# A two-layer hybrid trunk on one core: low parts of the conv weights by ScalarE and an adding transfer, p·v of two heads in turns, and the work between the attention units spread anew

## The chip, the cores and the metric

The kernel runs on one core of one Trainium2 chip. The metric is the device time of one execution in microseconds: 1858.16 us, the median of three runs (1857.69 to 1860.25). Engines are named as the profile names them: PE is TensorE (matrix products; PEld is its loading of weights), DVE is VectorE, ACT is ScalarE, POOL is GpSimd, SP issues the loads. Each engine takes its instructions in the order of its own queue. "Granted clock" is the share of TensorE's full clock that the throttle lets through: 1.00 is 2.4 GHz and 0.50 is 1.2 GHz.

## The reference

A sequence of 512 tokens of width 1024 goes through two layers. Each layer is: SwiGLU half step, a mixer, SwiGLU half step, each with an RMSNorm before it, shift and scale from a conditioning vector, and a gated residual add. All data are float32. The two mixers are the places of the change:

```
def conv_mixers(h, w_in, conv_a_w, conv_a_b, ln_a_g, ln_a_b, conv_b_w, w_out):   # layer 0
    z = h @ w_in                                      # 1024 x 2560
    a_val, a_gate, b_gate, c_gate, b_val = split(z)   # 512 columns each
    a = a_val * sigmoid(a_gate)
    a = causal_depthwise_conv(a, conv_a_w) + conv_a_b # 31 taps
    a = silu(group_layer_norm(a, 8, ln_a_g, ln_a_b))
    bb = b_gate * causal_depthwise_conv(c_gate * b_val, conv_b_w)   # 3 taps
    return concatenate([a, bb]) @ w_out

def pool_moba_mixers(...):                            # layer 1
    u, q, k, v = split(h @ w_in)                      # 512 columns each, 8 heads of 64
    pooled = multiscale_pool(u, ...)                  # trailing means of 2, 4, 8, 16 and a 128x128 product
    att = moba_attention(q, k, v)                     # causal softmax(q k' - slope * distance) v
    return concatenate([pooled, att]) @ w_out
```

With 512 tokens and blocks of 256 each query sees all keys before it, so the attention is plain causal attention with a linear bias.

## The kernel before

Activations lie transposed, channels on the 128 partitions and the 512 tokens along the row. A weight tile of 128x1024 (an **item**: 128 output columns, 8 steps over the inputs) is split into a high part, its rounding to the short float type that TensorE takes at full rate, and a low part, the rest. Each step of a product is then three matmuls of 128x512 into one PSUM bank (`mac`, L299 to L301): high times high, high times low of the activations, low times high. One item is 24 matmuls.

`run` walks a plan that is written out by hand. Before the step that uses item n it emits the splits of up to three items ahead (`AHEAD`), as far as the ring of four weight buffers (`W_BUFS`) allows. `split` has two instructions: ACT rounds the raw tile (`whi`, L284), and DVE subtracts (`wlo <- raw - whi`, L286); for items marked `pool_low` POOL subtracts. Raw tiles are loaded by SP (`load`, L268 or L261) into four buffers, each with two items.

**The conv stage** (`build`): items z[0] to z[3] belong to the step across the norm before it; then come z[3] to z[19] one after the other, each followed by `conv_tick`, which emits five taps of the 31-tap convolution on DVE (L1126, one multiply-add each) and three on ACT and POOL (ACT multiplies, `tp`, L1114, three buffers; POOL adds, L1115). The order of the items is sigmoid gate and value (`ag`, `av`) of four channel groups, then for two pairs of groups `cg`, `bv`, `bgate`. What an item leaves behind is put to DVE and ACT too: `bv` multiplies (`cb`, L1051), ACT makes the first of three taps (`yb`, L1054), DVE the two others (L1058). The normalisation over groups of 64 channels (`group_norm`) goes in three steps over PE, DVE, ACT and POOL (L1166 to L1192). After z[19] the first four items of the output product (`zo[0]` to `zo[3]`) are done step by step: steps 4 and 5 of each item, then 6, 7, 0, 1, 2, 3 of all four. Of these, zo[1] to zo[3] are `pool_low`.

**The attention stage**: 8 heads of 4 query blocks are 32 units. Unit n emits the scores of its block (two matmuls, L1345 and L1346, softmax on DVE and ACT), the transposes of the probabilities of unit n-3 (L1372, copied by ACT to `pta` and `ptb`, two buffers each), and, where unit n-6 was the last of a head, that head's product p·v (`product`, L1393: four float32 matmuls of 64 output rows, 512, 384, 256 and 128 columns; even heads write rows 0 to 63 of a bank, odd heads rows 64 to 127). After two heads ACT and DVE split the bank into high and low part for the output product. Between the units stand other matmuls, so that PE has work while a softmax runs: `FILL` says in which units half an item of the input product stands (12 matmuls), `PARTS` in which units steps of the first four output items stand.

Of the kernel before, what the change touches and what calls it, by code (L numbers as in the profile page):

```python
# [8 lines left out]
F32 = mybir.dt.float32  # L9
# [5 lines left out]
P = 128  # L15
D = 1024
S = 512
# [25 lines left out]
class Item:  # L43


    def __init__(self, raw, cut, shape, post=None, rhs=None, korder=None, store=None):
        self.raw, self.cut, self.shape = raw, cut, shape
        self.post, self.rhs = post, rhs
        self.korder, self.store = korder, store
        self.hi = self.lo = self.ps = None  # L50
        self.left = 0
        self.pool_low = self.late = self.hold = False


class Pair:
# [13 lines left out]
class Trunk:  # L69
# [183 lines left out]
    def load(self, r):  # L253
        n = 1
        for s in r.shape[1:]:
            n *= s
        t = self.raw.tile([P, 2048], F32, name="raw", tag="raw")[:, 0:n]
        if isinstance(r.src, tuple):
            r.tile = t.rearrange("p (g k c) -> p g k c", g=2, k=ND)
            for g in range(2):  # L260
                self.nc.sync.dma_start(r.tile[:, g], r.src[g])  # L261
        elif len(r.shape) == 4:
            r.tile = t.rearrange("p (a b c) -> p a b c", a=r.shape[1], b=r.shape[2])
            for b in range(r.shape[2]):
                self.nc.sync.dma_start(r.tile[:, :, b, :], r.src[:, :, b, :])
        else:
            r.tile = t.rearrange("p (a b) -> p a b", a=r.shape[1])
            self.nc.sync.dma_start(r.tile, r.src)  # L268

    def split(self, it):  # L270
        nk, m = it.shape
        src = it.cut(it.raw.tile)
        if it.store is None:
            parts = [[p.tile([P, 1024], F32R, name=n, tag=n)[:, 0:nk * m].rearrange(
                "p (a b) -> p a b", a=nk) for p, n in ((self.wp, "whi"), (self.wp, "wlo"))]]
            step = nk
        else:
            parts = [[t.rearrange("p (a b) -> p a b", b=m) for t in pair] for pair in it.store]
            step = S // m
        it.hi, it.lo = [], []  # L280
        for i, (hi, lo) in enumerate(parts):
            w = src[:, i * step:(i + 1) * step, :]
            n = w.shape[1]
            self.nc.scalar.copy(hi[:, 0:n, :], w)  # L284
            eng = self.nc.gpsimd if it.pool_low else self.nc.vector
            low = lambda eng=eng, lo=lo, hi=hi, w=w, n=n: eng.tensor_tensor(  # L286
                lo[:, 0:n, :], w, hi[:, 0:n, :].bitcast(F32), op=ALU.subtract)
            if it.hold:
                self.held.append(low)
            else:  # L290
                low()
            it.hi += [hi[:, a, :] for a in range(n)]
            it.lo += [lo[:, a, :] for a in range(n)]
# [350 lines left out]
    def t_rhs(self, k):  # L644
        return self.th[k], self.tl[k]

    def pair(self, src, nk, posts, apart=False, **kw):
# [4 lines left out]
        r = Raw([P, nk, 256], src, 2)  # L652
        return [Item(r, (lambda t, j=j: t[:, :, j * P:(j + 1) * P]), (nk, P), post=posts[j], **kw)
                for j in range(2)]

    def ffn_items(self, l, s):
        nc, a = self.nc, self.a
# [360 lines left out]
    def conv_items(self):  # L1018
# [53 lines left out]

        def two(c0, fn, jp):
            return self.pair(w[:, :, c0 + jp * 256:c0 + (jp + 1) * 256], ND, [fn(2 * jp), fn(2 * jp + 1)],
                             rhs=self.h_rhs)
        z = []
        for jp in range(2):
            g, v = two(512, ag, jp), two(0, av, jp)
            z += [g[0], v[0], g[1], v[1]]
        for jp in range(2):  # L1080
            z += two(1536, cg, jp) + two(2048, bv, jp) + two(1024, bgate, jp)
        wo = a["conv_w_out"][0].rearrange("(k p) f -> p k f", p=P)
        return z, self.out_items(wo, 1)

# [247 lines left out]
    def att_units(self):  # L1332
# [30 lines left out]
        def turn(h, c):  # L1363
            def go():
                p, _ = pr.pop((h, c))
                n = c + 1
                if c == 0:
                    pt[h] = (self.fp.tile([P, 2, S], F32, name="pta", tag="pta", bufs=2),
                             self.fp.tile([P, 2, 256], F32, name="ptb", tag="ptb", bufs=2))
# [9 lines left out]
                self.free(ps)  # L1379
            return go  # L1380

        def product(h):
            def go():
                j, r = h // 2, 64 * (h % 2)
                if h % 2 == 0:
                    self.oT[j] = self.bank()
                po = self.oT[j]
                for kt in range(4):
                    if kt < 2:
                        rhs = pt[h][0][:, kt, kt * P:S]  # L1390
                    else:
                        rhs = pt[h][1][:, kt - 2, (kt - 2) * P:256]
                    nc.tensor.matmul(po[r:r + 64, kt * P:S], lhsT=self.v[kt][:, h * HD:(h + 1) * HD],  # L1393
                                     rhs=rhs, start=kt == 0, stop=kt == 3, skip_group_check=True)
                if h % 2 == 1:
                    nc.scalar.copy(self.th[4 + j], po)

                    def low():
                        nc.vector.tensor_tensor(
                            self.tl[4 + j], po, self.th[4 + j].bitcast(F32), op=ALU.subtract)  # L1400
                        self.free(po)
                    self.defer(low)
            return go

        us = [(h, c) for h in range(NH) for c in range(4)]
        steps = []
        for n in range(len(us) + LAG):
            fns = []
            if n >= LAG and us[n - LAG][1] == 3:
                fns.append(product(us[n - LAG][0]))  # L1410
            if 3 <= n <= len(us) + 2:
                fns.append(turn(*us[n - 3]))
            if n < len(us):
                fns.append(score(*us[n]))
# [124 lines left out]
    def build(self):  # L1539
# [113 lines left out]
        bg = steps(1, (2, 0), (2, 2))  # L1653
        for n, fns in enumerate(units):
            self.call(lambda fns=fns: [fn() for fn in fns])
            if 1 <= n < len(FILL) and bg:
                self.call(*bg.pop(0)[:2])
            if n < len(FILL) and FILL[n]:
                for _ in range(FILL[n]):
                    self.part(*halves.pop(0))  # L1660
            elif n in PARTS:
                for e, k in PARTS[n]:
                    self.outer([lead[e]], k, None, k == 0, False)
            else:
                self.call(self.tick)
        self.call(self.flush)
        self.call(lambda: self.table(AF.Silu))
        self.outer(lead, 7, None, False, True)
# [35 lines left out]
JOIN = 1  # L1704
LAG = 6
FILL0 = 1
FILL = (2,) + (1,) * 21


def lead_parts(*steps):  # L1710
# [64 lines left out]
```

## Time and profile before

| | |
|---|---|
| median of the runs | 1858.16 us |
| profiled execution, its own time | 1858.03 us |
| its span, first to last instruction | 1856.1 us |
| PE busy | 1804.8 us (97%) |
| DVE busy | 1436.5 us (77%) |
| ACT busy | 800.4 us (43%) |
| POOL busy | 133.9 us (7%) |
| conv stage after the norm, from z[3] to the end of the output steps | 423.6 to 557.3 us |
| attention units | about 1324 to 1467 us |

A busy time counts an instruction from its start to its end. PE's matmuls overlap each other, so the distance between the starts of two matmuls tells what one costs, and an idle time of PE is the sure sign of a wait. What ended an idle time stands behind it as the releaser. A share over the whole span hides what a single stage waits for, so the stages are read one by one.

### The profile page before, as it was taken

How to read it: one execution, taken by the hardware profiler on the slowest of the kernel's cores; microseconds unless marked ns; L12 is line 12 of the kernel's file. 1: busy time of each engine (PE TensorE's matmuls, PEld its weight loads, DVE VectorE, ACT ScalarE, POOL GpSimd, SP SyncE). 2: the span in 40 equal slices, each digit the busy share in tenths (PEclk: the TensorE clock that was granted, in tenths of full speed). 3: DMA queues.
4: the chain of work that ended last, by engine and by line, in shares of the span. 5: the costliest groups of instructions: out<-in, count | busy, mean ns of one | idle time of the engine just before them, and what ended most of it. 6: DMA issues, size and time to landing. Idle time of an engine off the chain costs nothing.

```text
span 1856.1 us, 26640 instructions
## 1 busy us (share of the span) xinstructions
PE 1804.8 (97%) x10730; PEld 1568.3 (84%) x10730; DVE 1436.5 (77%) x2100; ACT 800.4 (43%) x1388; POOL 133.9 (7%) x107
## 2 busy tenths in 40 slices
PE   5999999999979999999999999999999999999998
PEld 4787889988758888989888889998876688898997
DVE  6689779788987869889678787886898576485874
ACT  4322335445543433535343334463545444253543
POOL 2100000005550000000000000000002000000000
PEclk7999999999989999999999999999999999999999
DMA  9585563433233346353423574533462132424321
GB/s 257 166 290 200 169 202 105 137 114 114 69 114 114 111 139 204 116 157 114 149 79 114 196 219 130 157 124 108 132 206 77 46 92 67 115 80 126 91 91 46
DMA packets 263234, 247.52 MB, mean 133 GB/s; under 512 B 5212, under 2 KB 243656, under 8 KB 263112
## 3 DMA queue, kind: packets, MB, share of 16 engines
q1 hardware_dynamic: 262980, 245.78, 42.8%
q8 instruction: 84, 1.38, 0.3%
q14 instruction: 38, 0.31, 0.1%
q10 hardware_dynamic: 132, 0.05, 0.0%
HBM read 243.72 MB, written 2.10 MB: 132 GB/s over the span
## 4 chain that ended last, share of the span: by engine, by line
PE 86%; DVE 9%; ACT 2%; issue 1%; POOL 1%; DMA 1%; SPq 0%; ACTq 0%; DVEq 0%; POOLq 0%
PE bank L784 30%; PE bank L299 17%; PE bank L301 17%; PE bank L300 17%; DVE hl L577 1%; DVE bank L1126 1%; DVE wlo L286 1%; PE bank L1393 1%; DVE t L572 1%; DVE acc L1516 1%; PE bank L1346 1%; PE bank L1372 1%; DVE adaacc L484 1%; ACT whi L284 1%; DVE x L1003 1%
## 5 line engine op out<-in xcount | busy, mean ns | idle before, releaser
L299 PE MATMUL bank<-th,whi 128*128 128x512 f32 (+1 forms) x896 | 337.4, 377 | 5.1 <-ACT whi L284 4.5
L301 PE MATMUL bank<-th,wlo 128*128 128x512 f32 (+1 forms) x896 | 333.6, 372 | 5.4 <-POOL wlo L286 5.4
L300 PE MATMUL bank<-tl,whi 128*128 128x512 f32 (+1 forms) x896 | 333.6, 372 | 1.1 <-DVE tl L680 0.9
L299 PE MATMUL bank<-hh,whi 128*128 128x512 f32 (+1 forms) x864 | 322.0, 373 | 5.4 <-ACT hh L575 3.2
L300 PE MATMUL bank<-hl,whi 128*128 128x512 f32 (+1 forms) x864 | 316.2, 366 | 8.0 <-DVE hl L577 8.0
L301 PE MATMUL bank<-hh,wlo 128*128 128x512 f32 (+1 forms) x864 | 315.2, 365 | 2.5 <-DVE wlo L286 2.5
L284 ACT CAST whi<-raw 128x1024 fp32r<-128x1024 f32 (+1 forms) x205 | 203.9, 1011 | 136.3 <-PE bank L300 83.3
L286 DVE TENSOR_TENSOR wlo<-raw,whi 128x1024 fp32r<-128x1024 f32 (+1 forms) x195 | 234.6, 1220 | 25.0 <-ACT whi L284 24.2
L301 PEld LDWEIGHTS bank<-th,wlo 128*128 128x128 f32 x896 | 169.6, 189 | 38.3 <-POOL wlo L286 6.6
L299 PEld LDWEIGHTS bank<-th,whi 128*128 128x128 f32 x896 | 169.6, 189 | 37.8 <-ACT whi L284 5.6
L300 PEld LDWEIGHTS bank<-tl,whi 128*128 128x128 f32 x896 | 169.7, 189 | 32.0 <-DVE tl L680 1.3
L300 PEld LDWEIGHTS bank<-hl,whi 128*128 128x128 f32 x864 | 163.6, 189 | 37.5 <-DVE hl L577 9.5
L299 PEld LDWEIGHTS bank<-hh,whi 128*128 128x128 f32 x864 | 163.6, 189 | 37.2 <-ACT hh L575 3.3
L301 PEld LDWEIGHTS bank<-hh,wlo 128*128 128x128 f32 x864 | 163.7, 189 | 31.9 <-DVE wlo L286 3.7
L1003 DVE SCALAR_TENSOR_TENSOR x<-bank,modG,x 128x512 f32<-128x512 f32 (+1 forms) x124 | 85.7, 698 | 133.2 <-PE bank L301 132.3
L784 PE MATMUL bank<-f,qhi 128*128 128x256 f32 x896 | 165.3, 282 | 0.0
L784 PE MATMUL bank<-f,whi 128*128 128x256 f32 x896 | 163.0, 280 | 0.1
L741 ACT CAST qhi<-raw 128x512 fp32r<-128x512 f32 x168 | 100.5, 619 | 111.9 <-issue 76.9
L484 DVE SCALAR_TENSOR_TENSOR adaacc<-raw,cond,adaacc 128x1024 f32<-128x1024 f32 x112 | 143.6, 1282 | 2.9 <-DMA raw<-in_ada_w_dram 0.2
L784 PEld LDWEIGHTS bank<-f,whi 128*128 128x128 f32 x896 | 137.7, 188 | 1.9 <-ACT yy L844 0.9
L784 PEld LDWEIGHTS bank<-f,qhi 128*128 128x128 f32 x896 | 138.8, 191 | 0.0
L784 PE MATMUL bank<-f,qlo 128*128 128x256 f32 x448 | 126.6, 283 | 0.2 <-DVE qlo L744 0.2
(245 smaller groups left out, 3323.6 us busy)
## 6 DMA issues: line engine op xcount, KB each, us to landing
raw<-in_ada_w_dram SPq DMA_DIRECT2D x64, 1024.0 KB, 5.4
raw<-in_ffn_w_down_dram SPq DMA_DIRECT2D x32, 1024.0 KB, 5.5
raw<-in_ffn_w_gate_dram SPq DMA_DIRECT2D x58, 512.0 KB, 4.1
raw<-in_ffn_w_up_dram SPq DMA_DIRECT2D x58, 512.0 KB, 5.3
raw<-in_ffn_w_gate_dram SPq DMA_DIRECT2D x15, 1024.0 KB, 5.7
raw<-in_ffn_w_up_dram SPq DMA_DIRECT2D x15, 1024.0 KB, 5.4
raw<-in_ffn_w_down_dram SPq DMA_DIRECT2D x16, 768.0 KB, 4.6
raw<-in_conv_w_in_dram SPq DMA_DIRECT2D x10, 1024.0 KB, 5.3
```

The costliest lines, as they stand in the source:

```text
L284: self.nc.scalar.copy(hi[:, 0:n, :], w)
L286: low = lambda eng=eng, lo=lo, hi=hi, w=w, n=n: eng.tensor_tensor(lo[:, 0:n, :], w, hi[:, 0:n, :].bitcast(F32), op=ALU.subtract)
L299: nc.tensor.matmul(ps, lhsT=it.hi[k], rhs=xh[:, sl], start=start, stop=False)
L300: nc.tensor.matmul(ps, lhsT=it.hi[k], rhs=xl[:, sl], start=False, stop=False)
L301: nc.tensor.matmul(ps, lhsT=it.lo[k], rhs=xh[:, sl], start=False, stop=stop)
L484: nc.vector.scalar_tensor_tensor(acc, r.tile[:, j, :], self.cond[:, k:k + 1], acc, op0=ALU.mult, op1=ALU.add)
L572: nc.vector.scalar_tensor_tensor(t, self.x[k][:, sl], self.modA[:, i, k:k + 1], rb, op0=ALU.mult, op1=ALU.mult)
L577: self.pend = lambda: nc.vector.scalar_tensor_tensor(self.hl[k][:, sl], t, b, self.hh[k][:, sl].bitcast(F32), op0=ALU.add, op1=ALU.subtract)
L741: self.nc.scalar.copy(hi, src)
L784: mm = lambda w, x, start=False: nc.tensor.matmul(ps, lhsT=w, rhs=x, start=start, stop=False, skip_group_check=True)
L1003: nc.vector.scalar_tensor_tensor(self.x[d][:, sl], ps[:, sl], self.modG[:, i, d:d + 1], self.x[d][:, sl], op0=ALU.mult, op1=ALU.add)
L1126: nc.vector.scalar_tensor_tensor(st[e], ap[:, t:t + S], weight(t), st[e], op0=ALU.mult, op1=ALU.add)
```

## The change

Three things change. First, the 16 conv items z[4] to z[19] get their low part another way: ACT writes the negative of the raw tile to `wlo` (it is rounded to the short type on the way), and a transfer issued by POOL adds the raw tile to it. For that the two items of a raw tile lie one behind the other (`whole`), and each raw tile of the conv input weights is loaded by two DMAs of 512 KB. Second, `product` takes a pair of heads and alternates between them, matmul by matmul; `pta` and `ptb` get three buffers. Third, `FILL` and `PARTS` are other tables, and a unit may now have both.

```
             eng = self.nc.gpsimd if it.pool_low else self.nc.vector
             low = lambda ...: eng.tensor_tensor(lo, w, hi, op=ALU.subtract)
-            if it.hold:
+            if it.by_dma:
+                self.nc.scalar.activation(lo[:, 0:n, :], w, AF.Copy, scale=-1.0)
+                self.nc.gpsimd.dma_start(lo[:, 0:n, :], w, accum_op=ALU.add)
+            elif it.hold:
                 self.held.append(low)
...
+        if whole:
+            r = Raw([P, 2, nk, P], (src[:, :, 0:P], src[:, :, P:2 * P]), 2)
+            cuts = [lambda t, j=j: t[:, j] for j in range(2)]
...
+        for it in z[4:]:
+            it.by_dma = True
...
-        def product(h):
+        def product(j):
             def go():
-                j, r = h // 2, 64 * (h % 2)
-                if h % 2 == 0:
-                    self.oT[j] = self.bank()
-                po = self.oT[j]
+                po = self.bank()
                 for kt in range(4):
-                    ...
-                    nc.tensor.matmul(po[r:r + 64, kt * P:S], lhsT=self.v[kt][:, h * HD:(h + 1) * HD], ...)
+                    for e in range(2):
+                        h, r = 2 * j + e, 64 * e
+                        ...
+                        nc.tensor.matmul(po[r:r + 64, kt * P:S], lhsT=self.v[kt][:, h * HD:(h + 1) * HD], ...)
...
-            if n >= LAG and us[n - LAG][1] == 3:
-                fns.append(product(us[n - LAG][0]))
+            if n >= LAG and us[n - LAG][1] == 3 and us[n - LAG][0] % 2 == 1:
+                fns.append(product(us[n - LAG][0] // 2))
...
-FILL = (2,) + (1,) * 21
+FILL = (0, 0) + tuple(range(1, 21)) + (22,)
...
 PARTS = lead_parts(
-    (22, ((0, 1), (0, 1))), (23, ((2,), (0, 1))), (24, ((0, 1), (4,)), ((3,), (0, 1)), ((2, 3), (4,))),
-    (26, (ALL, (5,))), (28, (ALL, (2,))), (30, (ALL, (3,))), (34, (ALL, (6,))))
+    (24, ((0, 1), (0, 1))), (26, ((2, 3), (0, 1))), (28, (ALL, (4,))), (30, (ALL, (5,))),
+    (31, (ALL, (2,))), (33, (ALL, (6,))), (35, (ALL, (3,))))
```

On POOL, at the start of the conv stage, this stood before (the subtraction and the small power of the norm, then the additions of the convolution, L1115):

```order
L286 TENSOR_TENSOR wlo<-raw,whi 128x1024
L554 TENSOR_TENSOR rs_163<-ms_161,mhalf 128x2
L1115 TENSOR_TENSOR y<-y,tp 128x512 x29
L1180 TENSOR_TENSOR grs<-gms,mhalf 128x8
L1115 TENSOR_TENSOR y<-y,tp 128x512 x11
```

And now, from the same power on (the additions are L1124 there, the adding transfers L290):

```order
L557 TENSOR_TENSOR rs_163<-ms_161,mhalf 128x2
L290 DMA wlo<-raw 128x1024 x3
L1124 TENSOR_TENSOR y<-y,tp 128x512 x2
L290 DMA wlo<-raw 128x1024
L1124 TENSOR_TENSOR y<-y,tp 128x512 x3
```

The transfers of z[4] to z[6] stand ahead of the first addition, and from then on one transfer stands behind every three additions, 16 in all; an addition behind it is issued only after it.

On ACT, in the middle of the conv stage, this stood before (three multiplications of taps, the rounding of an item, the copy of a `cg` item):

```order
L1114 ACTIVATE tp_4067<-ap1_3868,tapT_149 128x512
L1114 ACTIVATE tp_4070<-ap1_3868,tapT_149 128x512
L1114 ACTIVATE tp_4073<-ap1_3868,tapT_149 128x512
L284 CAST whi_4076<-raw_3807 128x1024
L1044 COPY cg_4105<-bank2_4080 128x512
```

And now:

```order
L1123 ACTIVATE tp_4083<-ap1_3877,tapT_149 128x512
L1123 ACTIVATE tp_4086<-ap1_3877,tapT_149 128x512
L1123 ACTIVATE tp_4089<-ap1_3877,tapT_149 128x512
L284 CAST whi_4092<-raw_3812 128x1024
L289 ACTIVATE wlo_4093<-raw_3812 128x1024
L1051 COPY cg_4122<-bank2_4097 128x512
```

One instruction of 128x1024 is added behind each rounding; on DVE the 16 subtractions of these items are gone, and no other instruction of the stage changes its place there.

On PE, at the first product p·v (unit 9), this stood before (the last matmul of a half item, the four products of head 0, and the transposes):

```order
L301 MATMUL bank_12692<-hh_104,wlo 128x512
L1393 MATMUL bank_12705<-pta,v_12573 64x512
L1393 MATMUL bank_12705<-pta,v_12578 64x384
L1393 MATMUL bank_12705<-ptb,v_12583 64x256
L1393 MATMUL bank_12705<-ptb,v_12588 64x128
L1372 MATMUL bank_12710<-ident,p 128x128 x3
```

And now, at unit 13, where both heads 0 and 1 are complete:

```order
L304 MATMUL bank_12861<-hh_104,wlo 128x512
L1402 MATMUL bank_12876<-pta,v_12599 64x512 x2
L1402 MATMUL bank_12876<-pta,v_12604 64x384 x2
L1402 MATMUL bank_12876<-ptb,v_12609 64x256 x2
L1402 MATMUL bank_12876<-ptb,v_12614 64x128 x2
L1381 MATMUL bank_12886<-ident,p 128x128 x3
```

The product of the even head has moved four units later and is interleaved with that of the odd head; the two of each "x2" write the two halves of the partitions of one bank.

## Rows read from the trace of the kernel before

**Rows 1.** The page: PE and granted clock, in 40 slices of the span.

```profile
PE   5999999999979999999999999999999999999998
...
PEclk7999999999989999999999999999999999999999
```

**Rows 2.** Stretches of the conv stage: length, busy us (instructions), clock, DMA share, GB/s.

```profile
424.00:526.00 102.00, 101.16 (x439) 80.60 (x438) 92.12 (x115) 59.03 (x86) 61.04 (x42) 1.00 0.27 88
526.00:557.30 31.30, 20.74 (x72) 14.56 (x71) 25.69 (x32) 13.87 (x21) 16.28 (x9) 0.73 0.38 134
529.80:540.10 10.30, 5.85 (x12) 3.65 (x12) 9.44 (x12) 3.44 (x5) 7.83 (x4) 0.50 0.30 102
543.50:550.30 6.80, 6.80 (x21) 5.09 (x21) 3.99 (x7) 2.67 (x4) 1.65 (x1) 0.50 0.83 308
```

**Rows 3.** Timeline of PE there: start, us, instruction, [idle before <-releaser].

```profile
530.56 0.79 PE L299 MATMUL bank<-th,whi 128*128 128x512 f32 x1 [4.02 <-ACT whi L284]
...
535.47 0.80 PE L301 MATMUL bank<-th,wlo 128*128 128x512 f32 x1 [3.69 <-POOL wlo L286]
```

**Rows 4.** Waits, 498 to 558 us: us in total, times, longest.

```profile
ACT yb L1054 <- DVE cb L1051: 7.0, 2, 4.7
...
PE bank L1166 <- POOL y L1115: 0.7, 1, 0.7
```

**Rows 5.** Groups by line, 424 to 526 us: busy, mean ns, idle before.

```profile
L1115 POOL TENSOR_TENSOR y<-y,tp 128x512 f32<-128x512 f32 x40 | 58.3, 1458 | 50.4 <-ACT tp L1114 48.3
...
L286 DVE TENSOR_TENSOR wlo<-raw,whi 128x1024 fp32r<-128x1024 f32 x17 | 27.5, 1625 | 6.0 <-ACT whi L284 6.0
```

**Rows 6.** Groups by line, whole span: POOL and the subtraction on DVE.

```profile
L286 DVE TENSOR_TENSOR wlo<-raw,whi 128x1024 fp32r<-128x1024 f32 (+1 forms) x195 | 234.6, 1220 | 25.0 <-ACT whi L284 24.2
...
L286 POOL TENSOR_TENSOR wlo<-raw,whi 128x1024 fp32r<-128x1024 f32 x10 | 23.7, 2370 | 22.9 <-ACT whi L284 22.9
...
L554 POOL TENSOR_TENSOR rs<-ms,mhalf 128x2 f32<-128x2 f32 x12 | 8.4, 700 | 1495.3 <-DVE ms L553 1495.3
L1180 POOL TENSOR_TENSOR grs<-gms,mhalf 128x8 f32<-128x8 f32 x4 | 7.6, 1889 | 13.6 <-DVE gms L1178 13.6
```

**Rows 7.** DMA issues: KB each, median us from issue to landing.

```profile
raw<-in_conv_w_in_dram SPq DMA_DIRECT2D x10, 1024.0 KB, 5.3
raw<-in_ada_w_dram SPq DMA_DIRECT2D x16, 512.0 KB, 7.9
...
out_dram<-yo SPq DMA_DIRECT2D x8, 256.0 KB, 2.5
```

**Rows 8.** Timeline of SP's queue, one issue.

```profile
515.99 0.37 SPq L268 DMA_DIRECT2D raw<-in_ada_w_dram  x1
```

**Rows 9.** Timelines at z[3] and z[4]: ACT first, then PE.

```profile
423.42 2.00 ACT L284 CAST whi<-raw 128x1024 fp32r<-128x1024 f32 x2
...
423.62 0.39 PE L299 MATMUL bank<-hh,whi 128*128 128x512 f32 x1
...
429.21 0.39 PE L299 MATMUL bank<-hh,whi 128*128 128x512 f32 x1
...
429.68 0.39 PE L301 MATMUL bank<-hh,wlo 128*128 128x512 f32 x1
```

**Rows 10.** Timeline of PE at the product of head 0.

```profile
1363.07 0.40 PE L301 MATMUL bank<-hh,wlo 128*128 128x512 f32 x1
1363.40 1.72 PE L1393 MATMUL bank<-pta,v 128*64 128x512 f32 x4
...
1365.70 0.55 PE L1372 MATMUL bank<-ident,p 128*128 128x128 f32 x3
```

**Rows 11.** Stretches of the attention units, columns as in the second group.

```profile
1324.00:1369.00 45.00, 44.97 (x191) 33.07 (x191) 41.71 (x69) 22.02 (x48) 0.00 (x0) 1.00 0.71 239
1369.00:1427.00 58.00, 57.96 (x241) 39.71 (x239) 49.62 (x97) 28.94 (x71) 13.43 (x10) 1.00 0.31 100
1427.00:1467.00 40.00, 39.58 (x165) 25.80 (x165) 21.34 (x51) 16.62 (x48) 0.00 (x0) 1.00 0.17 53
```

More of the change, by code (lines that the diff above doesn't have):

```diff
@@ L51, in __init__ @@
         self.left = 0
-        self.pool_low = self.late = self.hold = False
+        self.pool_low = self.late = self.hold = self.by_dma = False
 class Pair:
@@ L258, in load @@
         if isinstance(r.src, tuple):
-            r.tile = t.rearrange("p (g k c) -> p g k c", g=2, k=ND)
+            r.tile = t.rearrange("p (g k c) -> p g k c", g=2, c=P)
             for g in range(2):
@@ L645, in t_rhs, with pair @@
         return self.th[k], self.tl[k]
-    def pair(self, src, nk, posts, apart=False, **kw):
+    def pair(self, src, nk, posts, apart=False, whole=False, **kw):
         if apart:
@@ L651, in pair @@
                          post=posts[j], **kw) for j in range(2)]
-        r = Raw([P, nk, 256], src, 2)
-        return [Item(r, (lambda t, j=j: t[:, :, j * P:(j + 1) * P]), (nk, P), post=posts[j], **kw)
-                for j in range(2)]
+        if whole:
+            r = Raw([P, 2, nk, P], (src[:, :, 0:P], src[:, :, P:2 * P]), 2)
+            cuts = [lambda t, j=j: t[:, j] for j in range(2)]
+        else:
+            r = Raw([P, nk, 256], src, 2)
+            cuts = [lambda t, j=j: t[:, :, j * P:(j + 1) * P] for j in range(2)]
+        return [Item(r, cuts[j], (nk, P), post=posts[j], **kw) for j in range(2)]
     def ffn_items(self, l, s):
@@ L1074, in two @@
             return self.pair(w[:, :, c0 + jp * 256:c0 + (jp + 1) * 256], ND, [fn(2 * jp), fn(2 * jp + 1)],
-                             rhs=self.h_rhs)
+                             rhs=self.h_rhs, whole=True)
         z = []
@@ L1367, in go @@
                 if c == 0:
-                    pt[h] = (self.fp.tile([P, 2, S], F32, name="pta", tag="pta", bufs=2),
-                             self.fp.tile([P, 2, 256], F32, name="ptb", tag="ptb", bufs=2))
+                    pt[h] = (self.fp.tile([P, 2, S], F32, name="pta", tag="pta", bufs=3),
+                             self.fp.tile([P, 2, 256], F32, name="ptb", tag="ptb", bufs=3))
                 ps = self.bank()
@@ L1380, in turn, with low @@
             return go
-        def product(h):
+        def product(j):
             def go():
-                j, r = h // 2, 64 * (h % 2)
-                if h % 2 == 0:
-                    self.oT[j] = self.bank()
-                po = self.oT[j]
+                po = self.bank()
                 for kt in range(4):
[L1389 to L1402, printed above, removed]
+                    for e in range(2):
+                        h, r = 2 * j + e, 64 * e
+                        if kt < 2:
+                            rhs = pt[h][0][:, kt, kt * P:S]
+                        else:
+                            rhs = pt[h][1][:, kt - 2, (kt - 2) * P:256]
+                        nc.tensor.matmul(po[r:r + 64, kt * P:S], lhsT=self.v[kt][:, h * HD:(h + 1) * HD],
+                                         rhs=rhs, start=kt == 0, stop=kt == 3, skip_group_check=True)
+                nc.scalar.copy(self.th[4 + j], po)
+                def low():
+                    nc.vector.tensor_tensor(
+                        self.tl[4 + j], po, self.th[4 + j].bitcast(F32), op=ALU.subtract)
+                    self.free(po)
+                self.defer(low)
             return go
@@ L1655, in build @@
             self.call(lambda fns=fns: [fn() for fn in fns])
-            if 1 <= n < len(FILL) and bg:
+            if 1 <= n and bg:
                 self.call(*bg.pop(0)[:2])
[L1658 to L1664, printed above, removed]
+            for _ in range(FILL.count(n)):
+                self.part(*halves.pop(0))
+            for e, k in PARTS.get(n, ()):
+                self.outer([lead[e]], k, None, k == 0, False)
+            if n not in FILL and n not in PARTS:
                 self.call(self.tick)
+        assert not halves
         self.call(self.flush)
```

## The prediction

> **What bounds the kernel now.** I read the page's slices first: PE is busy in nearly all of them, and outside the first slice the granted clock falls in one place only, slices 11 and 12, which are the end of the conv stage [rows 1]. So a gain must come either from there or from less work on PE. Then the stretches: up to 526 us PE runs through (101.16 of 102 us), while DVE is busy for 92.12 of them, and in the 31.3 us after it PE works for 20.74 us only [rows 2]. The two longest gaps, 4.02 and 3.69 us, end with a rounding by ACT and a subtraction by POOL [rows 3]. Neither is slow; both are late, because their queues stood behind DVE: ACT's `yb` waited up to 4.7 us for DVE's `cb` [rows 4], and POOL was idle for 50.4 of the 102 us, 48.3 of them for ACT's `tp` [rows 5]. The chain is DVE late, hence ACT late, hence POOL late, hence PE idle. In the attention stage there is nothing of that kind: PE is busy for 142.5 of 143 us [rows 11]. What it can lose there is work.
>
> **Conv stage: what is removed.** DVE gives up 16 of the 17 subtractions of the stretch to 526 us, at 1625 ns each [rows 5] 26 us. Its 92.1 us fall to 66 in a stage in which PE needs about 100, so it is no longer late. What PE lost by it: 31.30 - 20.74 = 10.6 us idle after 526 us [rows 2], 0.7 us before that at the norm's product, which waited for POOL's sum [rows 4], and the clock. Two stretches ran at 0.50, the 1.2 GHz level, with 5.85 and 6.80 us of work, 12.65 us [rows 2]; before them PE had stood idle for 4.02 us, and within the first one for 3.69 us [rows 3]. At 1.00 that work takes half, so 6.3 us come back. Together 10.6 + 0.7 + 6.3 = 17.6 us can be won.
>
> **Conv stage: what is added.** ACT gets 16 more instructions of 128x1024. Two roundings of that size take 2.00 us [rows 9], so 16 us: its 59 us of the stretch become 75 of about 98 [rows 2]. That fits, and each stands right behind its rounding. POOL gets 16 issues of a transfer. No row shows one, so I bound the issue: below by SP's issue of a load, 0.37 us [rows 8], above by POOL's own subtraction of such a tile, 2.37 us [rows 6]. Between them lie POOL's two instructions with hardly any data, 0.70 and 1.89 us [rows 6]; I take 1.2, nearer to the first. Per item POOL then has three additions of 1.46 us [rows 5] and one issue, 5.6 us, and PE takes 429.21 - 423.62 = 5.6 us for an item [rows 9]. This is just in balance, and a split is emitted three items, 16.8 us, before its use; I count the delay of POOL's queue at nothing as long as an issue stays under about 2 us. Behind the transfer wait POOL's additions, for those ACT's `tp`, and behind these the next rounding: that is the way on which a long issue would come back to PE.
>
> The subtraction took 1625 ns here and 1220 ns over the whole span [rows 5, 6], and the difference is found where POOL's additions run. The Trainium skill (SBUF — State Buffer, "Who interferes with whom") says that a DVE instruction with two inputs in SBUF and a POOL instruction that reads SBUF block each other. By that rule the additions get shorter too when the subtractions go: if POOL regains the 0.4 us of each, its 43 additions take 1.3 us instead of 1.46, and the issue may take 1.7 us without any delay. By the row alone it is 1.2 us. The sum is the same by both.
>
> The transfer has to land. The nearest rows are an output of 256 KB, 2.5 us, and a load of 512 KB in short runs, 7.9 us [rows 7]; an adding transfer of 512 KB reads two tiles, so I take the 1 MB load's 5.3 us. Within 16.8 us that is hidden for all items but the first. z[4] is used early: its rounding starts at 423.42 [rows 9], the negative ends about 425.4, and with 1.2 and 5.3 us the low part is there at 431.9 at the latest (430.7 if the 5.3 us hold the issue), while PE wants it at 429.68 [rows 9]. Cost 1 to 2.2 us, I take 1.5; with the bounds of the transfer -0 to 5. At the end I leave 1.8 us of waits that stay (POOL still subtracts for zo[1] to zo[3] at 2.37 us each, and the norm's chain is as it was). The load in two DMAs of 512 KB instead of one of 1 MB I cost at nothing: it is cover of the same size as above, and the DMA share is 0.27 [rows 2]; without cover one more issue is 0.37 us. Sum of the conv stage: 17.6 - 1.5 - 1.8 = 14.3 us won.
>
> **The products p·v.** One head takes PE from 1363.40 to 1365.70, 2.30 us, for 2560 columns (each of the four products is done in two passes), and getting in costs 0.1 us more than a normal distance of 0.23 after 1363.07 [rows 10]; I allow as much for getting out. A pair costs 2 x 2.30 + 0.4 = 5.0 us. In turns, the two heads use different halves of the output rows. If PE works on both halves at once, the second head runs one pass behind the first: 2.30 + 0.46 (512 of 2560 columns) + 0.2 = 2.96, a gain of 2.0 us per pair and 8.2 us for four. If not, only one way in and out goes, 0.8 us in all. No row shows two neighbouring matmuls on different halves, so these are the bounds, and below nothing if each change of half cost 0.1 us: 4 x 7 x 0.1 = 2.8 us lost. I take the upper one, less 0.7 us because DVE is busy for 41.71 of 45 us up to 1369 [rows 11] and may become the wait while PE gets faster there: 7.5 us.
>
> **The new tables.** The number of matmuls is the same, so only waits could go, and there are 0.5 us [rows 11]. I count zero. If a unit without fill now starved, the softmax (DVE 21 of 40 us in the last stretch, [rows 11]) would show up as gaps of PE; bounds -0.5 to +2.
>
> **Sum.** The profiled execution took 1858.03 us, a span of 1856.1 and 1.9 us around it; the median of the runs is 1858.16, the same for this purpose. 1858.0 - 14.3 - 7.5 = 1836 us.
>
> **Rivals.** (B) PE does not work on both halves at once: 1858.0 - 14.3 - 0.8 = 1843 us. For it: no row shows it, and PE takes its matmuls in order. Against it: the products are narrow, 64 of 128 columns of weights [rows 10]. The Trainium skill speaks on both sides: TensorE: Matmul & The Clock Gate, "Part 3: Packing small matmuls", says that matmuls on different column groups run together (three of them 2.38 times as fast), and in the same section that weights are loaded beside a running matmul only where the row group differs, which here it does not. By its first rule (A) follows, by its second (B); no run here shows either.
>
> (C) An issue on POOL takes 2 to 2.5 us. Then POOL falls behind by about 1 us per item, some 10 us at the end, the same lag as DVE's now, and half of the conv gain is lost: 1844 with overlapping products, 1850 without.
>
> (D) Slower: POOL's queue becomes the bound. From z[4] on it must do 43 additions (62.8 us), two powers (3.8), 13 issues X and the subtraction for zo[1] (2.4) before PE can go on, which today is at 535.5 us [rows 3, 5, 6]. From 430.5 us, a little after z[3]'s end at 429.2 [rows 9], 430.5 + 69.0 + 13 X = 535.5 gives X = 2.8 us: from there on the conv stage gets longer than now, and from 3.4 us on the products' gain is used up too. At X = 4.5 it is 22 us, 1858 + 22 - 7.5 = 1873 us, more if PE's gaps bring its clock down. For it: no row shows the issue. Against it: POOL's longest row for a whole tile is 2.37 us.
>
> (E) The change does not do what it says: the transfers land so late that PE waits for each one, and what DVE gives back is taken again. About 1858 us. Against it: 16.8 us of lead and a DMA share of 0.27 [rows 2].
>
> **Chances.** Forecast (A) 0.45, own range 1829 to 1842; B 0.22; C 0.15; D 0.10; E 0.08. A difference under 0.2% (3.7 us) cannot be told from none here. Faster takes A, B and C: 0.82; within 0.2% most of E: 0.07; slower D and the rest: 0.11. The range 1828 to 1856 takes in A, B and C with their bounds and a part of E, and leaves out D, the rest of E and 0.03 below.
>
> **What would show it.** Conv stage: no gap of PE over 2 us and no half clock between 520 and 557 us, DVE under 75% there, POOL's issues about 1.2 us, one gap of PE at z[4]'s third matmul. Attention: a pair of products about 3 us long with starts of the two heads interleaved (B: 4.8 us). I am wrong if POOL stays busy without a break through the stage and PE waits for its transfers, or if new gaps of PE stand in the units 21 to 37.

## The result, and the profile after

The changed kernel takes 1843.24 us (median of 6 runs, 1841.12 to 1845.51) against 1859.02 us before (6 runs on the same chip, 1857.69 to 1860.26): ratio 0.9915, interval 0.9903 to 0.9927, so 15.8 us faster. The forecast was 1836 us; the range held the time. Its profiled execution took 1845.38 us, span 1843.6, 12.5 us under the span before. It is one of three runs at 1844.8 to 1845.5 (mean granted clock 0.989 to 0.990); the other three took 1841.1 to 1841.7 (0.992 to 0.993), and what they did better has no trace.

Where these 12.5 us went is read between the first products behind four boundaries, rows of PE that both kernels have (start, us, instruction, the idle time before it and what ended it): into and out of the conv stage, then into and out of the attention stage. The kernel before:

```profile
405.58 0.40 PE L300 MATMUL bank<-hl,whi 128*128 128x256 f32 x1 [1.50 <-DVE hl L577]
...
593.66 0.38 PE L300 MATMUL bank<-hl,whi 128*128 128x256 f32 x1 [1.60 <-DVE hl L577]
...
1301.63 0.39 PE L300 MATMUL bank<-hl,whi 128*128 128x256 f32 x1 [1.50 <-DVE hl L577]
...
1495.40 0.39 PE L300 MATMUL bank<-hl,whi 128*128 128x256 f32 x1 [1.60 <-DVE hl L577]
```

The changed kernel:

```profile
406.31 0.39 PE L303 MATMUL bank<-hl,whi 128*128 128x256 f32 x1 [1.50 <-DVE hl L580]
...
583.49 0.38 PE L303 MATMUL bank<-hl,whi 128*128 128x256 f32 x1 [1.59 <-DVE hl L580]
...
1291.83 0.39 PE L303 MATMUL bank<-hl,whi 128*128 128x256 f32 x1 [1.60 <-DVE hl L580]
...
1482.70 0.38 PE L303 MATMUL bank<-hl,whi 128*128 128x256 f32 x1 [1.60 <-DVE hl L580]
```

The conv stage lasts 177.2 us (188.1 before) and the attention stage 190.9 (193.8): 10.9 and 2.9 us. Everything else is 1.3 us longer, spread over stages that weren't changed: 0.7 of it lies ahead of the first boundary. In the thirteen traces used here that boundary lies between 403.6 and 406.5 us, though the work up to it is the same, so single executions differ by as much without any change.

**Conv stage.** The changed kernel's stretches (length, busy us and instructions of PE, PEld, DVE, ACT, POOL, clock, DMA share, GB/s), which answer to [rows 2]:

```profile
424.70:525.50 100.80, 100.11 (x435) 79.66 (x435) 72.51 (x107) 78.00 (x108) 73.22 (x60) 1.00 0.78 174
525.50:547.50 22.00, 18.63 (x80) 13.75 (x79) 19.62 (x25) 9.89 (x15) 14.80 (x7) 0.84 0.56 192
529.50:536.40 6.90, 6.13 (x13) 4.14 (x14) 6.21 (x6) 3.65 (x6) 6.26 (x3) 0.51 0.45 152
```

DVE is down from 92 to 72.5 us (66 had been worked out; the stretch now holds four more taps and two more `yb`) and ACT up from 59 to 78 (75 had been worked out). One stretch at half clock is left, 6.9 us with 6.1 us of work. The waits of PE that stay, which answer to [rows 3]:

```profile
431.57 0.50 PE L304 MATMUL bank<-hh,wlo 128*128 128x512 f32 x1 [0.69 <-DMA wlo<-raw]
...
530.27 0.80 PE L304 MATMUL bank<-th,wlo 128*128 128x512 f32 x1 [2.66 <-POOL wlo L286]
...
547.09 0.66 PE L1195 MATMUL bank<-ident,sq 128*128 128x128 f32 x4 [0.71 <-ACT sq L1191]
```

The first is the forecast wait for z[4]'s transfer. The second is the low part of zo[1], which POOL still subtracts itself. The third belongs to the norm's chain; the kernel before has it too, with 0.69 us. The groups by line up to 525 us (busy, mean ns, idle before):

```profile
L1124 POOL TENSOR_TENSOR y<-y,tp 128x512 f32<-128x512 f32 x42 | 58.4, 1390 | 22.2 <-ACT tp L1123 20.1
...
L289 ACT ACTIVATE wlo<-raw 128x1024 fp32r<-128x1024 f32 x16 | 16.9, 1058 | 0.0
L290 POOL DMA_DIRECT2D wlo<-raw x16 | 14.3, 892 | 19.2 <-ACT wlo L289 18.2 <-ACT sgm L1034 0.8
```

An issue of the adding transfer takes POOL 0.89 us, where 1.2 was taken. POOL at the end of the stage:

```profile
509.46 4.02 POOL L1124 TENSOR_TENSOR y<-y,tp 128x512 f32<-128x512 f32 x3 [4.30 <-ACT tp L1123]
513.42 0.89 POOL L290 DMA_DIRECT2D wlo<-raw  x1
514.03 5.58 POOL L1124 TENSOR_TENSOR y<-y,tp 128x512 f32<-128x512 f32 x3
519.57 1.67 POOL L1189 TENSOR_TENSOR grs<-gms,mhalf 128x8 f32<-128x8 f32 x1
523.18 4.73 POOL L1124 TENSOR_TENSOR y<-y,tp 128x512 f32<-128x512 f32 x3 [1.94 <-ACT tp L1123]
527.87 7.93 POOL L286 TENSOR_TENSOR wlo<-raw,whi 128x1024 fp32r<-128x1024 f32 x3
```

From 509 us to the end of the subtractions at 535.8 it has no break but one, and the three subtractions, 2.64 us each, stand behind the last additions.

**Attention stage.** The first pair of products, answering to [rows 10]:

```profile
1371.68 0.40 PE L304 MATMUL bank<-hh,wlo 128*128 128x512 f32 x1
1372.01 1.73 PE L1402 MATMUL bank<-pta,v 128*64 128x512 f32 x8
1373.56 0.82 PE L1402 MATMUL bank<-ptb,v 128*64 128x256 f32 x8
1374.31 0.55 PE L1381 MATMUL bank<-ident,p 128*128 128x128 f32 x3
```

Two heads take 1372.01 to 1374.31, 2.30 us: just what one took alone. Over four pairs PE has 4 x 2.30 = 9.2 us less to do. But the stage is only 2.9 us shorter, for the units have gaps now. First the stretches, 143 us in all as in [rows 11], then the larger gaps:

```profile
1314.20:1359.20 45.00, 43.81 (x189) 32.81 (x188) 41.77 (x68) 22.06 (x48) 0.00 (x0) 1.00 0.70 237
1359.20:1417.20 58.00, 56.32 (x250) 39.03 (x251) 52.14 (x105) 29.67 (x73) 13.42 (x10) 1.00 0.32 102
1417.20:1457.20 40.00, 37.38 (x170) 26.24 (x171) 21.37 (x50) 17.96 (x50) 0.00 (x0) 0.96 0.17 53
```

```profile
1359.07 0.66 PE L1381 MATMUL bank<-ident,p 128*128 128x128 f32 x4 [1.19 <-DVE p L1368]
...
1368.23 0.41 PE L1381 MATMUL bank<-ident,p 128*128 128x128 f32 x2 [1.22 <-DVE p L1368]
...
1419.22 0.38 PE L1354 MATMUL bank<-k,hh 128*128 128x256 f32 x1 [1.71 <-DVE hh L1228]
```

With a fourth of 0.47 us these make 4.6 us; behind the last one seven or eight matmuls ran at half clock and lost about 0.2 us each, 1.6 us. Together 6.2 us, and 9.2 less 6.2 is what the stage gained. Why DVE is late is seen in its queue ahead of the second gap:

```profile
1362.43 2.60 DVE L487 SCALAR_TENSOR_TENSOR adaacc<-raw,cond,adaacc 128x1024 f32<-128x1024 f32 x2
1365.06 1.39 DVE L1228 SCALAR_TENSOR_TENSOR th<-bank,th 64x512 fp32r<-64x512 f32 x2
1366.48 0.56 DVE L1359 SCALAR_TENSOR_TENSOR p<-dist,bank 128x384 f32<-128x384 f32 x1
...
1367.73 0.35 DVE L1368 TENSOR_SCALAR p<-p,pm 128x256 f32<-128x256 f32 x1
```

The norm that PE waits for, the last row, stands behind a scaling step (`adaacc`, a part of a later shift or gate, worked out from the conditioning vector) and the q of two heads, which take 4 us. From the first row to the last DVE needs 5.65 us for this unit; PE takes 4.0 us for a unit with its fill and no product (from 1359.07 to the next transposes at 1363.10).

Both gaps of 1.2 us stand ahead of the first pair. Head 0's product, 2.30 us of PE, has moved from unit 9 to unit 13, so PE comes that much sooner to the transposes of units 10 and 12, while DVE has the same to do as before; the 2.41 us of gaps eat what the move gave there. The runs below bear this out: tables_alone, which leaves that product in unit 9, has neither gap, and conv_pairs and in_row, which move it too, have both.

### The profile page after: what moved, and what is told of

Its sections match the earlier page's. It is cut to its first block, busy times and chain, and to the rows that moved or that the text cites. A ratio compares the mean times of both kernels' runs of the same rounds, so it can differ in the third digit from the quotient of the medians.

```text
span 1843.6 us, 26711 instructions
## 1 busy us (share of the span) xinstructions
PE 1794.6 (97%) x10730; PEld 1563.4 (85%) x10730; DVE 1411.1 (77%) x2084; ACT 816.1 (44%) x1404; POOL 144.5 (8%) x123
## 3 DMA queue, kind: packets, MB, share of 16 engines
q0 software_dynamic: 2304, 8.39, 2.5%
## 4 chain that ended last, share of the span: by engine, by line
PE 81%; DVE 10%; ACT 3%; issue 2%; POOL 2%; DMA 1%; SPq 0%; ACTq 0%; POOLq 0%; DVEq 0%
PE bank L791 30%; PE bank L302 16%; PE bank L304 16%; PE bank L303 16%; DVE hl L580 1%; DVE wlo L286 1%; DVE adaacc L487 1%; DMA raw<-in_ada_w_dram 1%; ACT whi L284 1%; DVE t L575 1%; POOL y L1124 1%; DVE pm L1362 1%; DVE x L1010 1%; DVE p L1359 0%; DVE acc L1524 0%
## 5 line engine op out<-in xcount | busy, mean ns | idle before, releaser
L286 DVE TENSOR_TENSOR wlo<-raw,whi 128x1024 fp32r<-128x1024 f32 (+1 forms) x179 | 209.4, 1187 | 19.1 <-ACT whi L284 18.4
```

## The experiments

Stage lengths are read as above, from each kernel's trace; times are medians, ratios against the kernel before in the same set of runs. Eight of these kernels have the changed conv stage as it is, and it took 176.7 to 178.2 us in their traces; four have the changed attention stage, 190.9 to 191.7 us. Smaller differences between two traces tell nothing.

| run | us | ratio, interval | conv stage | attention stage |
|---|---|---|---|---|
| before | 1859.02 | | 188.1 | 193.8 |
| changed | 1843.24 | 0.9915 (0.9903 to 0.9927) | 177.2 | 190.9 |
| conv_alone | 1846.85 | 0.9943 (0.9931 to 0.9955) | 176.9 | 193.8 |
| pairs_alone | 1859.69 | 1.0008 (0.9999 to 1.0017) | - | - |
| tables_alone | 1859.94 | 1.0008 (0.9999 to 1.0017) | 189.4 | 195.1 |
| conv_pairs | 1846.01 | 0.9938 (0.9925 to 0.9951) | 177.0 | 192.5 |
| in_row | 1848.35 | 0.9944 (0.9931 to 0.9956) | 176.7 | 194.8 |
| ada_half | 1851.19 | 0.9956 (0.9943 to 0.9970) | 178.2 | 198.2 |
| fill21 | 1845.17 | 0.9926 (0.9913 to 0.9938) | 177.7 | 191.5 |
| leads23 | 1849.84 | 0.9953 (0.9940 to 0.9965) | 184.0 | 191.5 |
| taps6 | 1846.26 | 0.9936 (0.9924 to 0.9949) | 179.2 | 191.7 |
| z_pool | 1847.67 | 0.9941 (0.9928 to 0.9953) | 181.0 | 190.9 |
| att_dma | 1841.38 | 0.9909 (0.9895 to 0.9923) | 177.7 | 188.8 |
| att_dma6 | 1838.17 | 0.9888 (0.9871 to 0.9904) | 177.0 | 185.8 |

### The parts apart

conv_alone keeps the conv stage's edits and takes the attention stage back to before; pairs_alone and tables_alone each make one attention edit on the kernel before; conv_pairs is the changed kernel with the old tables:

```
-FILL = (0, 0) + tuple(range(1, 21)) + (22,)
+FILL = (2,) + (1,) * 21
 (and the old PARTS and loop)
```

> Only the conv stage is changed (low parts by ScalarE and an adding transfer, and the loads cut in two); products and tables of the attention stage are as before. Theory T (the conv stage gives 11 to 13 us, the attention stage's products give about 9 us and the new tables take 5 to 6 of them back): about 1846.5 us, ratio 0.9935. Rival R (the tables take nothing, the products are given back to DVE, which has no time left): the same here, 1846.5. Only if the two parts of the change act on each other would this differ from 1858 less the 10.9 us that the conv stage is shorter by in the trace.

> Only the products of two heads in turns, on the old tables of fill and parts, with three buffers for the transposed weights. T: the two heads run at the same time, a pair takes 2.3 us in place of 5, and the old tables leave DVE enough room: about 8 us faster, 1850 us (ratio 0.9957). R: DVE is busy for 93 of 100 us up to unit 8 anyway and takes most of it back: 2 to 4 us faster, 1855 us, and PE waits for DVE's softmax in units 7 to 13 as in the changed kernel.

> Only the new tables of fill and parts (and the scaling steps that go on past the fill); one head at a time as before. T: slower by 3 to 6 us, 1861 to 1864 us, with a gap of PE of 1 to 2 us before the scores of head 6, which now come right behind the half item that computes them, and half clock after it. R: no difference, 1857 to 1859, since the products leave PE busy long enough to cover DVE.

> The changed kernel with the old tables of fill and parts back. T: faster than the changed kernel by 3 to 6 us, about 1838 us (ratio to the kernel before 0.989). R: 1842 to 1847 us, no faster than the changed kernel, because without the new tables PE starves somewhere else in the units 8 to 37.

The conv stage's edits are worth 10.6 us (8.4 to 12.8) by themselves. My theory of the tables fell: the products alone win nothing, the tables alone win nothing, and the old tables in the changed kernel make it no faster. Without the new tables the two gaps of 1.2 us stay, and in place of the wait at head 6's scores PE starves in the last units, conv_pairs:

```profile
1357.83 0.66 PE L1381 MATMUL bank<-ident,p 128*128 128x128 f32 x4 [1.22 <-DVE p L1368]
...
1366.98 0.41 PE L1381 MATMUL bank<-ident,p 128*128 128x128 f32 x2 [1.20 <-DVE p L1368]
...
1427.56 0.63 PE L1381 MATMUL bank<-ident,p 128*128 128x128 f32 x4 [2.01 <-DVE p L1368]
...
1446.42 0.55 PE L1381 MATMUL bank<-ident,p 128*128 128x128 f32 x3 [1.66 <-DVE p L1368]
```

So the saved time of PE comes back as waits for DVE, early or late; the tables only choose where the later ones stand, and both edits together win the 2.9 us, some 1.3 of them with the old tables. (No trace stands behind the time of pairs_alone, so it has no stages here.)

### Does taking in turns let two heads run at once?

in_row has the same eight products at the same place, head by head:

```
-                for kt in range(4):
-                    for e in range(2):
+                for e in range(2):
+                    for kt in range(4):
```

> The changed kernel with the eight matmuls of a pair in a row, four of the one head and then four of the other, at the same place in the program. If it is the taking in turns that lets two heads run at once, a pair takes 4.5 us in place of 2.3, PE has 9 us more work, of which the waits for DVE cover 3 to 5: 1847 to 1849 us (ratio 0.994). If PE runs any two neighbours on different halves at once, only the last matmul of the one head lies beside the first of the other, 4.3 us. If the place alone did it (one way in and out for two heads), the time is that of the changed kernel, 1843.

The time is in the first case's range, the pair is not: 1370.84 to 1374.70, 3.86 us.

```profile
1370.84 1.72 PE L1402 MATMUL bank<-pta,v 128*64 128x512 f32 x4
1372.40 0.38 PE L1402 MATMUL bank<-ptb,v 128*64 128x256 f32 x1
1372.40 0.64 PE L1402 MATMUL bank<-pta,v 128*64 128x512 f32 x1
...
1372.94 0.27 PE L1402 MATMUL bank<-ptb,v 128*64 128x128 f32 x1
...
1374.70 0.55 PE L1381 MATMUL bank<-ident,p 128*128 128x128 f32 x3
```

At 1372.40 a product of the one head and one of the other start together, and this goes on for some passes, so it is the halves that let them run at once, and the turns give PE a neighbour on the other half all the time. The other head's first product, which starts at 1372.40, stands in the program behind the fourth product of the one head, whose last pass starts at 1372.94: here PE started a matmul ahead of one that comes before it, and it did so in all four pairs. The turns are worth 1.56 us per pair, 6.2 in all, of which 3.9 reach the stage.

### Is DVE late for its work or for its order?

ada_half puts the scaling steps into every second unit; fill21 moves the last half item from unit 22 to 21:

```
-            if 1 <= n and bg:
+            if n % 2 == 1 and bg:
```
```
-FILL = (0, 0) + tuple(range(1, 21)) + (22,)
+FILL = (0, 0) + tuple(range(1, 22))
```

> The changed kernel with a scaling step (two DVE instructions of 128x1024, 2.6 us) in every second attention unit only, not in each one. Theory T2 (in the units 7 to 13 of the changed kernel DVE has more work per unit than PE: 2.6 us of scaling, 1.2 of a subtraction, 2 of softmax against 4.8 us of PE, and PE's two gaps of 1.2 us there are DVE's lateness): both gaps go, and the attention stage gets 2 to 3 us shorter, about 1841 us (ratio to the kernel before 0.9905). Rival R2 (the softmax's chain of PE, DVE, ACT and DVE again is too long for one unit, however much DVE has to do): the gaps stay, 1843 us.

> The changed kernel with the last half item one unit earlier (unit 21 in place of 22), so that the scores of head 6 in unit 24 come three units behind it. T2: the gap of 1.71 us before these scores and the half clock behind it (3 us of it, some 1.7 us lost) go, 2 to 3.4 us faster, about 1840.5 us, unless unit 22, now with no fill, starves by as much. R2: PE stands idle by the same time in unit 22, since what it lacks in units 21 to 24 is work: 1843 us.

In ada_half the two gaps of 1.2 us are gone, which bears T2 out as to their cause; but the stage got 7.3 us longer. The steps now stand in later units, where DVE has the pooling branch too and PE little to do; 1.92 us of the gap below DVE itself waited for ACT's copies of `k`. Its PE, and the stretch around:

```profile
1415.35 1.09 PE L1381 MATMUL bank<-ident,p 128*128 128x128 f32 x4 [3.51 <-DVE p L1368]
```

```profile
1411.00:1434.00 23.00, 16.87 (x49) 11.50 (x48) 18.67 (x38) 12.10 (x30) 0.00 (x0) 0.70 0.13 44
```

In fill21 the wait for head 6's scores is gone and one of 3.21 us stands in its place, at 1417.54: R2 held there. Moving work only moves the wait.

### DVE relieved in the attention units

att_dma gives eight items there the way of the conv stage, att_dma6 six of them:

```
-            us += two(0, self.pool_post, jp)
+            us += two(0, self.pool_post, jp, whole=True)
...
+        for it in us + kq[6:]:        # att_dma: kq[4:] + us
+            it.by_dma = True
```

> The changed kernel with the way of the conv stage for eight items of the attention stage as well (k and q of the heads 4 to 7 and the four of the pooling branch): low parts by ACT's negative and an adding transfer, eight subtractions of 1.2 us off DVE's queue. T2 (DVE's work per unit sets the pace in the units 7 to 13): the gaps of 1.19 and 1.22 us and part of the waits at units 21 to 24 go, 2 to 4 us faster, about 1840 us. R2 (the chain of one softmax, which goes to ACT and back, sets it; ACT now has 1 us more per item in that chain): no change, 1843, or 1 to 2 us slower. DMA: the share of 0.69 in the first 45 us of the units rises by some 0.2, and PE waits for loads if that is too much.

> The changed kernel with adding transfers for six items of the attention stage (the four of the pooling branch and the last k and q), not for the two before them. T2: the two gaps of 1.19 and 1.22 us (units 9 and 11) stay away as in the run with eight items, since the subtractions that stood in DVE's queue there belong to the pooling branch's items; and the gap of 1.71 us at 1342.5 us, in which ScalarE waited for a load that came late behind two transfers, is gone or under 0.8: the attention stage 1.5 us shorter than with eight items, about 187.3 us, the kernel about 1840 us. Rival: the late load is due to the pooling branch's loads in two halves, not to the two transfers ahead of it; the gap stays, and the stage takes 188.8 to 189.5 us, 1841 to 1842 us.

With eight, the two gaps fell to one of 0.47 us, and a new one of 1.71 us stood at 1344.2, ended by ACT's copy `ptb`, which stood behind a rounding that had waited 3.70 us for its load; the DMA share of the first 45 us was 0.87. With six, stretches of the same 143 us:

```profile
1312.20:1357.20 45.00, 45.00 (x196) 34.02 (x194) 41.63 (x73) 26.21 (x52) 1.78 (x2) 1.00 0.76 228
1357.20:1415.20 58.00, 57.13 (x252) 39.73 (x252) 48.97 (x98) 33.63 (x79) 15.99 (x14) 1.00 0.61 164
1415.20:1455.20 40.00, 38.54 (x184) 27.38 (x183) 22.89 (x53) 19.86 (x50) 0.00 (x0) 1.00 0.17 53
```

PE has no gap over 0.25 us in the first 100 us, and no half clock behind the wait for head 6's scores, which is down to 0.87 us. The stage is 5.0 us shorter than in the changed kernel, 7.9 shorter than before. This is the fastest version: ratio 0.9888, some 5 us under the changed kernel, whose interval it just touches.

### What holds the end of the conv stage

z_pool lets POOL subtract in place of the transfers; leads23 gives zo[1]'s subtraction to DVE; taps6 does DVE's taps three items earlier:

```
-            it.by_dma = True
+            it.pool_low = True
```
```
-LEADS = (1, 2, 3)
+LEADS = (2, 3)
```
```
-TAPS1 = (5,) * 17
+TAPS1 = (6,) * 17
```

> The changed kernel with the low parts of z[4] on subtracted by POOL itself, 16 times 2.4 us, in place of ACT's negative and the adding transfer. By the sum of rival D in the prediction (430.5 + 69.0 + 13 X, with X = 2.4, is 530.5 us, 5 us ahead of where PE could go on before) the conv stage is no longer than before, but some 3 to 6 us longer than with the transfers: 1846 to 1849 us. The rival: POOL and DVE slow each other (a subtraction on DVE took 1.63 us there in place of 1.22), POOL's share comes to 100%, ACT's `tp` and the roundings are late, and the conv gain is lost as a whole or more: 1855 us and above.

> The changed kernel with the low part of zo[1] subtracted by DVE in place of POOL; zo[2] and zo[3] stay with POOL. Theory: the 2.66 us that PE still waits at the end of the conv stage are POOL's queue (three additions to 527.9, then three subtractions of 2.6 us in a row); with one of them on DVE, which had 1.3 us to do there, this gap falls to below 1 us, the half clock behind it does not come, and the stage gets 2 to 4 us shorter, about 1840.5 us. Rival: DVE is late there as well (its `yb` comes 1.2 us later, and ACT's `th` behind it), and PE waits as long for another tile: 1843 us or more.

> The changed kernel with six taps of the wide convolution on DVE per item of the conv stage in place of five, so that the 79 taps are done three items earlier. Theory T3 (the end of the conv stage is bound by DVE's queue there: one more subtraction of 1.2 us on it made the kernel 7 us slower in the run before; up to 525 us DVE has 28 of 101 us to spare): ACT's `yb` and `th` no longer wait for DVE, POOL's last additions come earlier and with them its subtractions, the gap of 2.66 us and the half clock go: 3 to 6 us faster than the changed kernel, about 1839 us (ratio 0.989). Rival R3: the taps now collide with the items in the middle, where an item takes 5.6 us and DVE's share rises from 72 to 80%, and the end is held by POOL alone, whose additions stay where they are: 1842 to 1846 us.

z_pool has POOL busy for 95.81 of 101 us, and PE goes on at 531.95, where the sum of rival D, 430.5 + 69.0 + 13 X with the measured 2.48 us, says 531.7. The two are nearer than they should be: z[3] starts 1.4 us earlier in this trace than in the one that the sum starts from, POOL's additions took 1375 ns in place of 1458, and POOL still stood idle for 5 us. So the sum is good to about 2 us. Even this way is 7 us better in the stage than DVE's subtractions were; the transfers are worth 3.8 us of the 10.9.

In leads23 the one subtraction took DVE 2.31 us beside POOL's additions, ACT's `th` and the roundings queued behind it came later, and 13.5 us ran at half clock:

```profile
534.00:547.50 13.50, 11.13 (x30) 7.58 (x29) 8.78 (x12) 6.32 (x10) 4.01 (x2) 0.50 0.41 155
```

In taps6 DVE was ahead and then stood still for the sum that POOL's additions build, with `yb` queued behind it:

```profile
516.97 0.22 DVE L1187 TENSOR_SCALAR gms<-bank 128x8 f32<-128x8 f32 x2
526.31 1.41 DVE L1148 TENSOR_TENSOR y<-y,bank 128x512 f32<-128x512 f32 x2 [9.12 <-POOL y L1124]
```

PE's wait for POOL's first subtraction fell to 0.85 us there, and a new one came, for a rounding that stood behind ACT's `th` and with it behind `yb`:

```profile
532.21 0.80 PE L302 MATMUL bank<-th,whi 128*128 128x512 f32 x1 [2.34 <-ACT whi L284]
```

Both of my theories on this end fell. DVE can't take more there, and PE gains nothing when DVE is earlier, as R3 had it. By these waits the additions of POOL, which follow ACT's `tp`, set the end, through POOL's own subtractions in the changed kernel and through DVE's sum in taps6. That is read from the traces and not shown by a run: fewer additions in the last items, or the same ones earlier, were not tried.

## Why the prediction was right or wrong

**Direction and mechanism: right.** Both gains come from where they were put, DVE's queue in the conv stage and the products on two halves; rivals B to E did not come about. The time alone doesn't say so: 1843.24 us lies 1.2 us outside A's own range and is the figure of B; it is in the wide range because that takes in the rivals. B is refuted by the 2.30 us; C and D by an issue of 0.89 us; E because PE waits for one transfer only. POOL's additions took 1.39 us, between the 1.46 of the row and the 1.3 that the prediction gave them if the subtractions went.

**Conv stage, 14.3 forecast, 10.9 measured.** The 17.6 us that could be won were sized rightly. z[4]'s wait was 0.69 us where 1.5 was taken. The step that failed is "At the end I leave 1.8 us of waits that stay": there are 2.66 and 0.71 us of idle time, and 6.1 us of work at half clock, which lose 3.1. With the 0.7 at z[4] that is 7.1 us, and 17.6 - 7.1 = 10.5, about what is measured. I had the row of it (POOL's subtractions of 2.37 us each) and priced them as if POOL came to them on time. In conv_alone this stretch kept its clock, and PE waited once for each of the three, the third time 1.12 us at 534.27:

```profile
528.70 0.50 PE L304 MATMUL bank<-th,wlo 128*128 128x512 f32 x1 [2.59 <-POOL wlo L286]
...
531.48 0.50 PE L304 MATMUL bank<-th,wlo 128*128 128x512 f32 x1 [1.12 <-POOL wlo L286]
```

The stage was as long. Of the eight traces of this stage four are at full clock throughout (176.7 to 177.7 us) and four have such a stretch (177.0 to 178.2). So the clock cost next to nothing of its own; POOL's rate did. "No gap of PE over 2 us and no half clock" was wrong for the same reason. "DVE under 75% there" holds up to 525 us (72%) and not from 520 to 557, where DVE is busy for 34.13 of 37 us; at 531.40 ACT's `th` has waited 3.80 us for its `yb`. DVE is no longer late in the stage as a whole, but at its end it is.

**Products, 7.5 forecast, 2.9 measured for the whole stage.** PE's part was undersized: I let the second head run one pass behind the first, and it runs beside it, 2.30 us per pair where 2.96 was forecast. The Trainium skill's two rules (TensorE: Matmul & The Clock Gate, "Part 3: Packing small matmuls") differed here: the trace agrees with the one on column groups, by a factor of 2.0; the one that lets weights be loaded beside a running matmul only from another row group would have held it up, and no hold-up shows. The step that failed is the allowance, "less 0.7 us because DVE is busy for 41.71 of 45 us": the rows of DVE were the right ones to look at, but 6.2 us were given back, not 0.7. The new tables, which I counted at zero, are not where it went: with the pairs they win some 1.6 us of the stage (192.5 to 190.9), without them they lose 1.3 (193.8 to 195.1). That the gaps of PE show DVE's queue is settled by ada_half (the gaps go when the work ahead goes) and by att_dma6 (they go, and the stage gets 5.0 us shorter, when it goes for good). "If new gaps of PE stand in the units 21 to 37" hit the largest loss, 1.71 us and the half clock at head 6's scores; the two gaps of 1.2 us stood at the transposes of units 10 and 12, where I had not looked for any, though the change itself takes head 0's product out of unit 9.

Little cancelled: both terms were too high, by 3.4 and 4.6 us (by this one trace, whose execution took 2.1 us more than the median). Within the second, 9.2 us less work of PE where 8.2 was forecast stands against 5.5 us more that were given back.

**What stays open:** what the three shorter runs of the changed kernel did better, and whether a table could win more at the end of the attention stage.

## What to carry to other kernels

When work leaves the bounding engine, compare the other engines' work per unit, not per stage, with what that unit then takes: a stage in which DVE is busy for 80% can hold units in which it is the bound. Moving such work to other units moves the wait; taking it off the engine (here by ACT's negative and an adding transfer, which cost POOL 0.89 us and ACT 1.06) removes it, as long as the transfers don't delay the loads beside them.

## What the runs showed of the hardware that was not expected

The starts of the two heads' products lie so close that two matmuls on different halves of the output rows behave as one: eight take 1.73 us where four took 1.72 [rows 10], their weight loads included. In in_row one of them even started ahead of its turn.

DVE and POOL slow each other. The one subtraction that DVE still does in the conv stage took 2.32 us at 516.13, and the three additions of POOL beside it and beside DVE's `yb` took 5.58 us in place of 4.02; in the attention units, with POOL idle, such a subtraction took 1.23 us (at 1359.99).

An adding transfer is dear for the DMA engines. The changed kernel's DMA queues from 424 to 530 us (packets, MB, share of 16 engines; q0 carries the 16 adding transfers, q1 the loads):

```profile
q0 software_dynamic: 2304, 8.39, 43.8%
q1 hardware_dynamic: 13425, 9.25, 31.1%
```

A megabyte of q0 held the engines for 5.2% of the stretch (43.8 / 8.39), one of q1 for 3.4%: 1.55 times as much. In the kernel before, with the loads alone in these 106 us, it was 2.9% (25.9% for 8.90 MB). The loads of 512 KB beside them took 6.6 us to land, those of 1 MB 5.3 before [rows 7]. In the conv stage nothing waited for a transfer but z[4]'s third product; in att_dma ACT's rounding waited 3.70 us for its load, and PE behind it.
